# Interleaving the first two output chunks of an FFN's last slice, and closer spacing of a normalisation chain

## The chip, the cores and the metric

The kernel runs on one core of one Trainium2 chip. The metric is the device time of one execution in microseconds (us), lower is better. Engines are named as in the profile: PE is the matrix engine (PEld its weight loads), DVE the vector engine, ACT the scalar engine, POOL the general-purpose engine, SP the queue that issues most DMAs.

## What is computed

One inference step of a two-layer backbone over 640 tokens (512 latent tokens and 128 context tokens) of width 1024, in float32. Each layer is: half-step SwiGLU FFN, token mixer, half-step SwiGLU FFN. The mixer of layer 0 is a Fourier mix between two projections, that of layer 1 is 16-head attention. Every sub-layer stands between two RMS norms:

```
def _half_ffn(x, m, k, g_pre, g_post, w1, w2):
    h = _modulated_prenorm(x, g_pre, m, k)             # rmsnorm(x) * (1 + scale) + shift
    gate, up = split(h @ w1)
    return x + 0.5 * gate_k * _rmsnorm((silu(gate) * up) @ w2, g_post)
```

So there are six sub-layers, numbered n = 0 to 5: FFN, Fourier mix, FFN, FFN, attention, FFN. The FFN's hidden width is 2816, that is 22 tiles of 128.

## The kernel before

**Data.** Activations are kept transposed, 128 features by tokens, eight chunks of 128 features. The 640 tokens are worked as two halves of 320. A float32 product is made of three matmuls: weights and activations are each split into a high part (ACT copies it to the fast float32 format, `hi`) and the rest (DVE subtracts it, `lo`), and `mm3` (L228 to L230) issues hi by hi, hi by lo and lo by hi. Weights come in units of 128x1024: a DMA into one of four `raw` buffers (L156), ACT's `hi` (L194), DVE's `lo` (L195). `unit(i)` returns unit i and sends up to three units ahead of it.

**FFN.** The first product is made for hidden tiles f = 0 to 21, tiles 0 to 3 plainly, tiles 4 to 21 with a Strassen-like scheme that takes both halves at once (`w1_fast`). Of the last two tiles, 20 and 21, only half 0 is made at that point; their half 1 comes later (`tail`), from weight mixes that `mix` splits (L215, L216 on a 128x1024 `raw`). For half 0 of a tile, DVE subtracts the last product (L627), multiplies by the SiLU (L628), and `hidden` splits the result into g: ACT L215 for the high part, DVE L216 for the rest. The second product runs over slices of hidden tiles, (0,4), (4,8), (8,12), (12,16) and the last, (16,22). For each slice, half and output chunk m, `w2` takes a PSUM bank that ACT has seeded with the earlier slices' sum (L663), runs the tiles of the slice through `mm3`, and ACT copies the bank back to `y` (L675). In the last slice a chunk takes six tiles, 18 matmuls, the last three of which need g of tile 21. The slice has six weight units of eight 128x128 blocks; chunk m uses blocks 6m to 6m+5. The order of an FFN's end is: fast tiles 20 and 21, both mixes, reload of x, half 0 of the last slice (chunks 0 to 7), the boundary of half 0, `tail` for both tiles, half 1 of the last slice, the boundary of half 1.

**Boundary.** After each half a generator (`chain`: `post`, then the next sub-layer's `pre`) does the norms beside PE's next work. It is advanced by a clock that counts matmuls: `tick` adds 441.6 ns for a group of three 320-column matmuls, and each `yield n` says that the next piece is to be issued n ns of that clock later. Such a number only places the piece in program order: engines take their queues in order, and a list scheduler orders the queues at build time by that order and by its own estimate of when operands are ready. `post` issues: a fold of the sum of squares (L454) 2000 ns after the boundary, 1800 later a matmul that sums over partitions (L462), DVE's L465 and POOL's power (L466), 2800 later (2200 for half 0 and after a mixer) a matmul that spreads the result (L471) and ACT's copy of it (L475), 1300 later four pieces for two chunks each: DVE multiplies y by the norm (L520) and adds it to x (L522), ACT squares x (L420, L423) and DVE adds the squares (L424). Then `pre` does the same again for the next norm: fold L454, sum L462, spread L471, copy L475, and four pieces that scale x (L496, L502, L504) and split it into the next sub-layer's h (L215, L216). `finish(half)` or a loop of `step` issues what is left at once where the next sub-layer needs it. In attention two groups of value products (`v_tiles` for quads 1 and 0, "score" banks) stand behind half 0's query and key products; between them the chain is stepped until its second norm is through.

The few lines that fix this:

```
            yield 2500                       # in post, between the four pieces, L527/L528
...
            for f in range(f0, f1):          # in w2
                u, a = self.w2_tile(s, m, f - f0)
                w = self.unit(base + u)
```

`issue_after(x)` and `behind_of(x, y)` make the instructions that are built inside them stand behind x (and y) on x's (and y's) engine; no semaphore goes with it.

Of the kernel before, what the change touches and what calls it, by code (L numbers as in the profile page):

```python
# [24 lines left out]
HALF = TOK // 2  # L25
DEPTH = 2
DFF = 2816
NF = DFF // P
# [13 lines left out]
SLICES = ((0, 4), (4, 8), (8, 12), (12, 16), (16, 22))  # L42
# [10 lines left out]
SPAN = ((0, HALF), (HALF, TOK))  # L53
# [56 lines left out]
class Kernel:  # L110
# [271 lines left out]
    def gain_of(self, layer, sub, post):  # L382
        a = layer * 120 + 72 + (24 if post else 0) + sub * NCH
        return self.vec[:, a : a + NCH]
# [123 lines left out]
    def post(self, layer, sub, half, acc, last):  # L508

        nc = self.nc  # L510
        lo, hi = SPAN[half]
        r = yield from self.inverse_rms(acc, 2800 if half and sub != 1 else 2200)
        final = type(r) is tuple
        r, rp = r if final else (r, r)
        acc = None
        for c in range(0, NCH, 2):
            with self.tc.high_priority() if c == NCH - 2 else ExitStack():
                t = self.pair(self.y, c, half)
                engine, rb = (nc.gpsimd, r) if final and c == 2 else (nc.vector, rp)
                engine.tensor_tensor(t, t, rb[:, :HALF].unsqueeze(1).to_broadcast([P, 2, HALF]), op=ALU.mult)  # L520
                x = self.xpair(layer * 3 + sub + 1, c, half)
                engine.tensor_tensor(x, x, t, op=ALU.add)  # L522
                if last:
                    queue = nc.scalar if final and c == 2 else nc.sync
                    queue.dma_start(out=self.io["x_out"][:, c : c + 2, lo:hi], in_=x)
                else:
                    acc = self.sum_square(acc, x)  # L527
            yield 2500  # L528
        yield 1000
        self.normed[half][0] = True  # L530
        return acc

    def ffn(self, layer, which, base, boundary):
# [5 lines left out]
        g, sums, kept, mixes = {}, {}, {}, {}  # L539
        quad = lambda t: t.rearrange("p (c t) -> p c t", c=4)  # L540

        def hidden(f, v, half):
            lo, hi = SPAN[half]
            self.split(g[f][:, 0, lo:hi], g[f][:, 1, lo:hi], v[:, :HALF])

        def w1(fs, half):
            for f in fs:
                if f not in g:
                    g[f] = self.ring(F32R).rearrange("p (a t) -> p a t", a=2)
            pss = []  # L550
            if len(fs) == 1 or n == half == 0:
                for f in fs:
                    for j in range(2):
                        w = self.unit(base + self.w1_at[f] + j)
                        with self.tc.issue_after(self.latest.ins):
                            pss.append(self.proj(w, lambda k: k * P, half, kind="score" if f == 2 else "main"))
            else:
                pss = self.multi([self.unit(base + self.w1_at[f] + j) for f in fs for j in range(2)], half)
            for i, f in enumerate(fs):
                gate, up = pss[2 * i], pss[2 * i + 1]  # L560
                s, v = self.temp("left"), self.temp("right")
                with self.tc.high_priority():
                    nc.scalar.activation(s[:, :HALF], gate[:, :HALF], AF.Silu)
                    nc.vector.tensor_tensor(v[:, :HALF], up[:, :HALF], s[:, :HALF], op=ALU.mult)
                    hidden(f, v, half)
                while self.later:
                    self.later.pop()()
# [36 lines left out]
        def w1_fast(f):  # L604

            g[f] = self.ring(F32R).rearrange("p (a t) -> p a t", a=2)
            late = f in LATE
            a, q = (self.temp("left")[:, :HALF] for _ in range(2))
            s, v = (self.temp("right")[:, :HALF] for _ in range(2))
            x, y, z = (self.bank(kind)[:, :HALF] for kind in ("main", "score", "main"))  # L610
            product(f, x, 0, 0, lambda k: self.h.chunk(k, 0), True)
            with high():
                nc.scalar.activation(a, x, AF.Copy)
            product(f, y, 1, 512, lambda k: part(2, k), True)
            with high():
                tt(q, y, a, op=ALU.subtract)
            product(f, z, 1, 0, lambda k: part(3, k), True)
            with high():
                tt(a, q, z, op=ALU.subtract)
            if not late:  # L620
                w = one(f, a, 2)
            product(f, x, 0, 512, lambda k: self.h.chunk(4 + k, 0), False)
            with high():
                nc.scalar.activation(s, x, AF.Silu)
            product(f, z, 2, 0 if late else 512, lambda k: part(4, k), False)
            with high():
                tt(v, q, z, op=ALU.subtract)  # L627
                tt(v, v, s, op=ALU.mult)  # L628
                hidden(f, v, 0)
            if late:  # L630
                kept[f] = a, q
            else:
                two(f, a, q, w, 3, 0)
# [8 lines left out]
        def two(f, a, q, w, unit, at):  # L642
            product(f, w, unit, at, lambda k: self.h.chunk(4 + k, 1), False)
            with high():
                nc.vector.scalar_tensor_tensor(out=q, in0=w, scalar=-1.0, in1=q, op0=ALU.mult, op1=ALU.subtract)  # L645
                nc.scalar.activation(q, q, AF.Silu)
                tt(a, a, q, op=ALU.mult)
                hidden(f, a, 1)
# [7 lines left out]
        seeded = {}  # L656
# [5 lines left out]
            with self.tc.high_priority():  # L662
                nc.scalar.activation(ps[:, :HALF], self.y[:, m, lo:hi], AF.Copy)  # L663

        def w2(s, half, m):
            f0, f1 = SLICES[s]
            lo, hi = SPAN[half]
            ps = seeded.pop((s, half, m), None) or self.bank()
            for f in range(f0, f1):
                u, a = self.w2_tile(s, m, f - f0)  # L670
                w = self.unit(base + u)
                self.mm3(ps[:, :HALF], w[0][:, a : a + P], w[1][:, a : a + P],
                         g[f][:, 0, lo:hi], g[f][:, 1, lo:hi], f == f0 and s == 0, f == f1 - 1, s > 0)
            with self.tc.high_priority():
                nc.scalar.activation(self.y[:, m, lo:hi], ps[:, :HALF], AF.Copy)  # L675
            if f1 == NF:
                acc[half] = self.weigh(layer, 2 * which, half, m, acc[half])
# [3 lines left out]
        for op, a, half in self.ffn_plan:  # L681
# [3 lines left out]
            if op == "w1":  # L685
                if not begun[half]:
                    self.finish(half)
                    begun[half] = True
                w1(a, half)
            elif op == "combine":  # L690
                combine(a)
            elif op == "fast":
                w1_fast(a)
            elif op == "mix":
                mixes[a] = self.mix()
            elif op == "tail":
                tail(a)
            elif op == "w2":
                w2(a[0], half, a[1])
                if a[0] < len(SLICES) - 1:  # L700
                    passed += 1
                    due = BEHIND[n] * passed // (2 * NCH * (len(SLICES) - 1))
                    self.behind(due - done)
                    done = due
            elif op == "x":
                self.new_x(n + 1)
                for c in range(NCH // 2):
                    src = self.spilled[c].rearrange("p (c t) -> p c t", c=2) if n else self.io["x"][:, 2 * c : 2 * c + 2, :]
                    nc.sync.dma_start(out=self.xs[n + 1][c], in_=src)
            else:  # L710
                boundary(half, acc[half])
# [620 lines left out]
```

## Time and profile before

| what | value |
|---|---|
| time, median of 3 runs | 2305.4 us (2303.74 to 2306.14) |
| the profiled execution: its own time, its span | 2303.3 us, 2301.5 us |
| PE busy | 2253.5 us, 98% of the span |
| DVE, ACT, POOL busy | 75%, 56%, 2% |
| TensorE clock granted, mean | 0.995 |
| DMA over the span | 120 GB/s, 39275 instructions in all |

The span runs from the first to the last instruction. A row of the trace's timeline gives the start and the duration in us, the engine, the line, the operation, output and inputs, shapes, how many instructions are merged (x), and in brackets how long the engine had been idle and what released it.

### The profile page before, as it was taken

How to read it: one execution, taken by the hardware profiler on the slowest of the kernel's cores; microseconds unless marked ns; L12 is line 12 of the kernel's file. 1: busy time of each engine (PE TensorE's matmuls, PEld its weight loads, DVE VectorE, ACT ScalarE, POOL GpSimd, SP SyncE). 2: the span in 40 equal slices, each digit the busy share in tenths (PEclk: the TensorE clock that was granted, in tenths of full speed). 3: DMA queues.
4: the chain of work that ended last, by engine and by line, in shares of the span. 5: the costliest groups of instructions: out<-in, count | busy, mean ns of one | idle time of the engine just before them, and what ended most of it. 6: DMA issues, size and time to landing. Idle time of an engine off the chain costs nothing.

```text
span 2301.5 us, 39275 instructions
## 1 busy us (share of the span) xinstructions
PE 2253.5 (98%) x15660; PEld 2209.0 (96%) x15660; DVE 1732.4 (75%) x3010; ACT 1277.9 (56%) x2468; POOL 41.2 (2%) x64
## 2 busy tenths in 40 slices
PE   7999999999999999999999999999999999999997
PEld 5999999999999999999999999998888999999997
DVE  5889888588788887858978888578667485766574
ACT  5445544565654554556545554668668654545544
POOL 0000000000000000000000000000000000000000
PEclk9999999999999999999999999999999999999999
DMA  8244443334333433343334443424333223322331
GB/s 304 93 136 155 157 129 119 138 96 136 106 114 113 147 121 127 123 153 110 104 126 133 154 127 101 154 75 155 109 97 101 74 74 101 110 92 83 101 111 74
DMA packets 80281, 278.12 MB, mean 121 GB/s; under 512 B 8801, under 2 KB 15201, under 8 KB 79969
## 3 DMA queue, kind: packets, MB, share of 16 engines
q1 hardware_dynamic: 78736, 273.97, 36.3%
q8 instruction: 122, 2.00, 0.4%
q10 hardware_dynamic: 1360, 1.64, 0.2%
q14 instruction: 63, 0.51, 0.1%
HBM read 264.04 MB, written 11.53 MB: 120 GB/s over the span
## 4 chain that ended last, share of the span: by engine, by line
PE 88%; ACT 3%; DVE 3%; DMA 3%; issue 1%; POOL 0%; DVEq 0%; SPq 0%; ACTq 0%; POOLq 0%
PE main L228 25%; PE main L229 25%; PE main L230 25%; PE score L229 3%; PE score L230 3%; PE score L228 3%; DMA raw<-in_w 2%; DVE lo L195 1%; ACT hi L194 1%; PE turn L1147 1%; PE sum L1163 1%; PE sum L471 1%; PE score L1121 1%; PE sum L462 1%; ACT left L1107 0%
## 5 line engine op out<-in xcount | busy, mean ns | idle before, releaser
L228 PE MATMUL main<-ring,hi 128*128 128x320 f32 x3872 | 1205.2, 312 | 8.8 <-ACT ring L215 7.7
L229 PE MATMUL main<-ring,hi 128*128 128x320 f32 x3872 | 1198.1, 310 | 0.2 <-DVE ring L366 0.2
L230 PE MATMUL main<-ring,lo 128*128 128x320 f32 x3872 | 1197.6, 310 | 0.0
L228 PEld LDWEIGHTS main<-ring,hi 128*128 128x128 f32 x3872 | 727.6, 188 | 15.5 <-ACT ring L215 9.8
L229 PEld LDWEIGHTS main<-ring,hi 128*128 128x128 f32 x3872 | 728.5, 188 | 1.3 <-DVE ring L366 0.4
L230 PEld LDWEIGHTS main<-ring,lo 128*128 128x128 f32 x3872 | 728.0, 188 | 0.0
L194 ACT ACTIVATE hi<-raw 128x1024 fp32r<-128x1024 f32 (+1 forms) x366 | 355.8, 974 | 439.7 <-PE main L229 356.2
L195 DVE TENSOR_TENSOR lo<-raw,hi 128x1024 fp32r<-128x1024 f32 (+1 forms) x366 | 408.4, 1117 | 146.5 <-ACT hi L194 144.9
L388 DVE SCALAR_TENSOR_TENSOR junk<-raw,wide 128x1024 bf16<-128x1024 f32 x256 | 312.6, 1221 | 14.8 <-DMA raw<-in_w_mod_t 12.2
L675 ACT ACTIVATE y<-main 128x320 f32<-128x320 f32 x320 | 137.1, 432 | 154.0 <-PE main L230 153.3
L663 ACT ACTIVATE main<-y 128x320 f32<-128x320 f32 x256 | 111.4, 439 | 33.2 <-DVE left L645 26.8
L228 PE MATMUL score<-ring,hi 128*128 128x320 f32 x416 | 128.7, 309 | 0.0
L230 PE MATMUL score<-ring,lo 128*128 128x320 f32 x416 | 128.5, 309 | 0.0
L229 PE MATMUL score<-ring,hi 128*128 128x320 f32 x416 | 128.5, 309 | 0.0
L424 DVE TENSOR_TENSOR total<-total,square 128x640 f32<-128x640 f32 x71 | 58.4, 824 | 85.2 <-ACT square L423 83.8
L195 DVE TENSOR_TENSOR lo<-sums,hi 128x1024 fp32r<-128x1024 f32 x72 | 88.0, 1222 | 43.8 <-ACT hi L194 43.8
L194 ACT ACTIVATE hi<-sums 128x1024 fp32r<-128x1024 f32 x72 | 76.3, 1060 | 32.4 <-DVE sums L180 17.9
L228 PE MATMUL main<-ring,ring 128*128 128x320 f32 x288 | 90.9, 316 | 0.0
L230 PE MATMUL main<-ring,ring 128*128 128x320 f32 x288 | 89.1, 309 | 0.0
L229 PE MATMUL main<-ring,ring 128*128 128x320 f32 x288 | 89.0, 309 | 0.0
L215 ACT ACTIVATE ring<-right 128x320 fp32r<-128x320 f32 x104 | 47.9, 469 | 55.3 <-DVE right L628 34.4
L229 PEld LDWEIGHTS score<-ring,hi 128*128 128x128 f32 x416 | 78.1, 188 | 0.0
(185 smaller groups left out, 2631.3 us busy)
## 6 DMA issues: line engine op xcount, KB each, us to landing
raw<-in_w SPq DMA_DIRECT2D x264, 512.0 KB, 3.6
raw<-in_w_mod_t SPq DMA_DIRECT2D x128, 512.0 KB, 4.1
raw<-in_qkv SPq DMA_DIRECT2D x26, 512.0 KB, 3.6
first<-in_w_mod_k SPq DMA_DIRECT2D x16, 512.0 KB, 9.1
spill<-ring SPq DMA_DIRECT2D x12, 640.0 KB, 3.6
ring<-spill SPq DMA_DIRECT2D x12, 640.0 KB, 8.3
raw<-in_bias SPq DMA_DIRECT2D x16, 448.0 KB, 3.3
raw<-in_four_in SPq DMA_DIRECT2D x8, 512.0 KB, 3.7
```

The costliest lines, as they stand in the source:

```text
L194: nc.scalar.activation(hi, raw[:, at], AF.Copy)
L195: nc.vector.tensor_tensor(lo, raw[:, at], hi.bitcast(F32), op=ALU.subtract)
L215: a = self.nc.scalar.activation(hi, src, AF.Copy)
L228: mm(out, whi, xhi, start=start, stop=False)
L229: mm(out, whi, xlo, start=False, stop=False)
L230: self.latest = mm(out, wlo, xhi, start=False, stop=stop)
L388: last = self.nc.vector.scalar_tensor_tensor(out=self.junk, in0=raw, scalar=1.0, in1=self.wide[:, cond, :], op0=ALU.mult, op1=ALU.mult, ac ...
L424: nc.vector.tensor_tensor(acc, acc, sq, op=ALU.add)
L462: nc.tensor.matmul(ps[:, j : j + 1], acc[0][:, t : t + P], self.mean, start=True, stop=True)
L471: self.spread = nc.tensor.matmul(ps[:, t : t + P], col[:, j : j + 1].to_broadcast([P, P]), self.ident, start=True, stop=True)
L663: nc.scalar.activation(ps[:, :HALF], self.y[:, m, lo:hi], AF.Copy)
L675: nc.scalar.activation(self.y[:, m, lo:hi], ps[:, :HALF], AF.Copy)
```

## The change

Three edits. `hidden` keeps its two split instructions in `self.hid`. In the last slice, chunks 0 and 1 of half 0 are interleaved: first tiles 16 to 20 of chunk 0, then tiles 16 to 20 of chunk 1, then tile 21 of chunk 0, then tile 21 of chunk 1; chunks 2 to 7 and half 1 keep their order. The first part is built inside `behind_of(*self.hid)`, so weight units sent in it (the slice's fourth, and the fifth) stand behind tile 21's two split instructions on ACT and DVE. In `post`, half 1 of an FFN (sub 0 and 2) has 1800 instead of 2500 between its four pieces.

```
-            yield 2500
+            yield 1800 if half and sub != 1 else 2500
...
-            self.split(g[f][:, 0, lo:hi], g[f][:, 1, lo:hi], v[:, :HALF])
+            self.hid = self.split(g[f][:, 0, lo:hi], g[f][:, 1, lo:hi], v[:, :HALF])
...
+        def w2_part(ps, s, half, m, fs):
             f0, f1 = SLICES[s]
             lo, hi = SPAN[half]
-            ps = seeded.pop((s, half, m), None) or self.bank()
-            for f in range(f0, f1):
+            for f in fs:
                 u, a = self.w2_tile(s, m, f - f0)
                 w = self.unit(base + u)
                 self.mm3(ps[:, :HALF], w[0][:, a : a + P], w[1][:, a : a + P],
                          g[f][:, 0, lo:hi], g[f][:, 1, lo:hi], f == f0 and s == 0, f == f1 - 1, s > 0)
+
+        def w2(s, half, m):
+
+            f0, f1 = SLICES[s]
+            lo, hi = SPAN[half]
+            fs = range(f0, f1)
+            if f1 == NF and half == m == 0:
+                with self.behind_of(*self.hid):
+                    for i in range(2):
+                        w2_part(seeded[s, half, i], s, half, i, fs[:-1])
+            ps = seeded.pop((s, half, m), None) or self.bank()
+            w2_part(ps, s, half, m, fs[-1:] if f1 == NF and half == 0 and m < 2 else fs)
```

## Rows read from the trace of the kernel before

**Rows 1.** The page's busy time of PE, share of the span and instructions.

```profile
PE 2253.5 (98%) x15660; PEld 2209.0 (96%) x15660; DVE 1732.4 (75%) x3010; ACT 1277.9 (56%) x2468; POOL 41.2 (2%) x64
```

**Rows 2.** PE's waits over the span: us in total, times, longest.

```profile
PE main L228 <- ACT ring L215: 8.0, 6, 2.0
```

**Rows 3.** Timeline of PE around the start of each FFN's last slice.

```profile
424.47 0.31 PE L230 MATMUL main<-ring,lo 128*128 128x320 f32 x1
426.15 0.41 PE L228 MATMUL main<-ring,hi 128*128 128x320 f32 x1 [1.38 <-ACT ring L215]
...
1012.88 0.41 PE L228 MATMUL main<-ring,hi 128*128 128x320 f32 x1 [1.23 <-ACT ring L215]
...
1455.51 0.48 PE L228 MATMUL main<-ring,hi 128*128 128x320 f32 x1 [1.90 <-ACT ring L215]
...
2239.18 0.41 PE L228 MATMUL main<-ring,hi 128*128 128x320 f32 x1 [1.26 <-ACT ring L215]
```

**Rows 4.** Timeline of DVE at the first of these starts.

```profile
422.42 0.48 DVE L627 TENSOR_TENSOR right<-left,main 128x320 f32<-128x320 f32 x1
423.97 1.22 DVE L195 TENSOR_TENSOR lo<-raw,hi 128x1024 fp32r<-128x1024 f32 x1 [1.07 <-ACT hi L194]
425.11 0.48 DVE L628 TENSOR_TENSOR right<-right,right 128x320 f32<-128x320 f32 x1
426.13 0.49 DVE L216 TENSOR_TENSOR ring<-right,ring 128x320 fp32r<-128x320 f32 x1 [0.54 <-ACT ring L215]
```

**Rows 5.** Timeline of ACT at the first of these starts.

```profile
422.88 1.06 ACT L194 ACTIVATE hi<-raw 128x1024 fp32r<-128x1024 f32 x1 [1.30 <-DMA raw<-in_w]
...
425.63 0.47 ACT L215 ACTIVATE ring<-right 128x320 fp32r<-128x320 f32 x1 [1.37 <-DVE right L628]
426.01 1.04 ACT L215 ACTIVATE ring<-raw 128x1024 fp32r<-128x1024 f32 x1
```

**Rows 6.** Windows of equal length: busy time and count by engine, PEclk, DMA share, GB/s.

```profile
426.50:429.50 3.00, 3.00 (x22) 2.92 (x21) 2.49 (x3) 3.00 (x7) 0.00 (x0) 1.00 0.50 165
1455.70:1458.70 3.00, 3.00 (x12) 3.00 (x12) 2.54 (x3) 1.97 (x3) 0.00 (x0) 0.50 0.51 167
1534.40:1537.40 3.00, 2.83 (x13) 2.84 (x14) 2.15 (x6) 0.89 (x2) 0.00 (x0) 0.50 0.48 153
```

**Rows 7.** Timeline of PE where attention takes up half 1.

```profile
1527.54 0.28 PE L462 MATMUL sum<-mean,total 128*128 128x1 f32 x2
...
1529.67 0.38 PE L471 MATMUL sum<-ident,col 128*128 128x128 f32 x1 [0.49 <-POOL col L466]
...
1533.74 0.42 PE L228 MATMUL main<-ring,hi 128*128 128x320 f32 x1 [1.95 <-ACT ring L215]
```

**Rows 8.** Timeline of DVE at the same place.

```profile
1524.13 0.49 DVE L454 TENSOR_TENSOR total<-total 128x320 f32<-128x320 f32 x1
...
1531.11 0.83 DVE L496 TENSOR_TENSOR y<-ring,rms 128x640 f32<-128x640 f32 x1 [0.80 <-ACT rms L475]
...
1533.28 1.23 DVE L195 TENSOR_TENSOR lo<-raw,hi 128x1024 fp32r<-128x1024 f32 x1
```

**Rows 9.** Timeline of ACT at the same place.

```profile
1527.74 1.06 ACT L194 ACTIVATE hi<-raw 128x1024 fp32r<-128x1024 f32 x1 [0.38 <-PE score L230]
1530.64 0.44 ACT L475 ACTIVATE rms<-sum 128x320 f32<-128x320 f32 x1 [1.84 <-PE sum L471]
```

**Rows 10.** Timeline at the boundary into the third FFN: DVE and PE.

```profile
1085.25 0.48 DVE L454 TENSOR_TENSOR total<-total 128x320 f32<-128x320 f32 x1
...
1085.94 0.30 PE L462 MATMUL sum<-mean,total 128*128 128x1 f32 x2
...
1088.31 0.38 PE L471 MATMUL sum<-ident,col 128*128 128x128 f32 x1 [0.93 <-POOL col L466]
```

**Rows 11.** Timeline at the boundary into the Fourier mix: DVE and PE.

```profile
497.77 0.49 DVE L454 TENSOR_TENSOR total<-total 128x320 f32<-128x320 f32 x1
...
498.41 0.24 PE L462 MATMUL sum<-mean,total 128*128 128x1 f32 x1
```

More of the change, by code (lines that the diff above doesn't have):

```diff
@@ L663, in seed @@
                 nc.scalar.activation(ps[:, :HALF], self.y[:, m, lo:hi], AF.Copy)
-        def w2(s, half, m):
+        def w2_part(ps, s, half, m, fs):
             f0, f1 = SLICES[s]
             lo, hi = SPAN[half]
-            ps = seeded.pop((s, half, m), None) or self.bank()
-            for f in range(f0, f1):
+            for f in fs:
                 u, a = self.w2_tile(s, m, f - f0)
```

## Prediction, made before the change was built or run

> **What bounds the kernel now.** I read the page first: PE is busy 98% of the span [rows 1], so a gain must come from PE's pauses or from a better clock, and work on DVE, ACT or the DMAs counts only where PE waits for it. The waits of PE come next: the largest group after start-up is L228 waiting for ACT's split (L215), 8.0 us in six waits [rows 2]. The timeline of PE places four of the six: the start of the last slice in each of the four FFNs, 1.38, 1.23, 1.90 and 1.26 us idle [rows 3]. The matmul that ends the idle time is the first that needs g of tile 21. A fifth, 1.95 us, is where attention takes up half 1 [rows 7].
>
> The idle time is counted from the modelled end of the matmul before, 0.31 us after its start [rows 3], while matmuls in a stream start 0.147 us apart (441.6 ns for three on the kernel's own clock). So a pause costs PE its idle time plus 0.16 us: 1.54, 1.39, 2.06 and 1.42, together 6.4 us, and 2.1 us in attention.
>
> The reason for the first four stands in the queues of DVE and ACT. At the first FFN, DVE has finished L627 by 422.9 and could do L628 at once, but L195 of a weight unit stands between them; it runs from 423.97 to 425.19, and only then come L628, the high part and the rest [rows 4]. That L195 waited for ACT's L194, and this for its DMA, at 422.88 [rows 5]. It is the slice's fourth unit, the one that the slice's first call of `unit` sends three ahead: blocks 24 to 31, wanted first by chunk 4. So a unit that is wanted four chunks later holds up tile 21.
>
> **Part 1, the interleaving.** It adds no matmul and removes none. PE has 15 matmuls (2.2 us) between the last product of tile 21 and the first use of its g; after the change it has 30, 4.4 us. In the first FFN the use falls due at 424.47 + 0.15 = 424.62 before, at 426.8 after. With the old queues the rest of g is there at 426.62 [rows 4]; the four pauses (1.39 to 2.06) are all shorter than the added 2.2 us. The interleaving alone thus covers all four. Chunk 0's bank is copied out 2.2 us later and chunk 1's at the same place in the order; the bank that chunk 0 gives back is wanted by chunk 4, two chunks (5.3 us) later.
>
> **Part 2, the fourth unit behind tile 21.** L628 then follows L627: it starts near 423.0, and by the spacings in the rows (0.52 to the high part, 0.50 to the rest, 0.49 long) g is complete at 424.5, 2.3 us ahead of the new use and even about in time for the old. What is late next: the unit's L194 and L195 move behind the split, so its low part ends near 425.7 in place of 425.19. It is wanted by chunk 4, at 422.4 + 4 x 2.65 = 433.0; 7 us are left. On SP's queue a load waits for this unit's raw buffer, that of the sixth unit (wanted by chunk 6, near 440), and behind it stand the next sub-layer's loads and the reload of x, all for users later still: 0.5 us more costs none of them. The fifth unit already ran behind the split. The mix of 1.04 us on ACT that follows the split [rows 5] may slip ahead of it, with as much on DVE as a unit's L195, 1.22 [rows 4]: inside the 2.3 us. I put the loss at 0. Parts 1 and 2 give 6.4 us.
>
> **The clock.** After the third pause, the longest, the granted clock is 0.5 (1.2 GHz, the lower of the two levels): 12 matmuls in 3 us; after attention's pause the same. After the first, shorter pause it stays at 1.00, with 22 matmuls [rows 6]. Such a stretch thus costs 10 matmuls of 0.147 us, 1.5 us. The pause gone, I expect the stretch gone with it: 1.5 us from the third FFN. The Trainium skill speaks against this, on its page "TensorE: Matmul & The Clock Gate", Part 1, "What's actually happening": there it is idleness of the whole window looked at that brings the lower clock back. By that rule a pause with work close on both sides is not the cause, and the sum would lack this term; the rows, in which the two falls stand right behind the two longest pauses, do not agree with it.
>
> **Part 3, 1800 for 2500.** The first, sum, spread and copy keep their places; the pieces of `post` stand at 7.9, 9.7, 11.5 and 13.3 us after the boundary (before: 7.9, 10.4, 12.9, 15.4), and the closing sum of `pre` at 17.9 in place of 20.7. No work is added. The chain stands 2.8 us earlier in program order; whether it runs earlier depends on DVE's fold (L454).
>
> In attention it can. The fold is done at 1524.6 [rows 8], but the sum runs at 1527.54 [rows 7]: it is due 20.7 after the boundary and the first group of value products ends at 14.1 + 5.65 = 19.8, so it comes behind them (32 groups of three at 0.4416 us for the products, 16 at 0.353 for the values), and spread, copy (1530.64 [rows 9]), L496 and the rest follow late. With 17.9 the sum falls inside that group, near 1527.54 - 1.9 = 1525.6, after the fold. POOL's power then runs beside matmuls, and the spread follows the group at once, some 1.4 us earlier than the 1529.67 of now. This can remove the 2.1 us pause, the 0.49 + 0.16 before the spread, and the half clock behind it (1.5): 4.2 us at most. Against the whole of it: the second value group needs the low part of a weight unit, whose L194 waits for PE to free a buffer (1527.74 [rows 9]) and whose L195 stands at 1533.28 in DVE's queue behind L496 [rows 8]. If L195 keeps its place behind L496 it ends 1.4 us earlier, like all behind the spread, while PE comes to it 1.1 us earlier, and most of the pause stays. But L195 could run from 1528.8, when its high part is there, and DVE sits idle for 0.80 us before L496 even now [rows 8]. Bounds 0 and 4.2; I take 3.0, nearer to the upper end, since a pause only a little shorter may already keep the clock.
>
> At the third FFN the fold ends at 1085.73, PE's sum follows at 1085.94, and the spread then waits 0.93 us for POOL [rows 10]; at the Fourier mix the fold ends at 498.26 and the sum follows at 498.41 without a wait [rows 11]. In both the sum already follows the fold closely, so the fold, not the interval, sets it. Earlier pieces let DVE finish the fold earlier by something up to 2.8 us, or not at all. No PE wait for h follows either. Gain at most 1.1 (the wait for POOL and its edge), loss see below; I take +0.3. In the last FFN nothing runs behind the chain, so the spacing places nothing.
>
> **The sum.** 6.4 + 1.5 + 3.0 + 0.3 = 11.2 us. The profiled execution took 2303.3 us, 1.8 more than its span, and lies 2.1 us under the median of the runs, just below the fastest of them (2303.74). Its own time becomes 2292.1, the median of runs 2305.4 - 11.2 = 2294.2.
>
> **The rivals.**
> *A. Attention's wait is only renamed.* The low part of the value unit takes the place of h, and the clock falls as before: 6.4 + 1.5 + 0.65 (the wait before the spread) = 8.55, 2296.9. For it: L195's place behind L496 [rows 8]. Against: DVE's half 0 work moves ahead too.
> *B. The earlier sums stall PE: slower than before.* PE takes its queue in order. If the sums at the Fourier mix and the third FFN are placed 2.8 us earlier and the folds end where they do now, PE waits 498.26 - 495.6 = 2.7 and 1085.73 - 1083.1 = 2.6 us, each long enough for a half-clock stretch as after the 1.90 and 1.95 us pauses: 2 x (2.65 + 1.5) = 8.3 against 7.9 gained, 2305.8, and more if DVE's fold is pushed back by the crowding. It decides from the point where both pauses reach 2.5 us. Against it: the queues' order puts both sums right behind the folds now, so the scheduler's estimate of the folds is good there, and DVE's pieces, issued earlier, should end earlier.
> *C. The first four pauses stay,* because something else than the fourth unit is late. Part 3 alone gives 3.3: 2302.1. Against: two independent covers.
> *D. The clock falls without the pauses,* at times of its own: neither the third FFN nor attention gets its 1.5 us back, 6.4 + 1.5 (part 3 without the clock) + 0.3 = 8.2, 2297.2. Against it: two falls, both behind a pause [rows 6, 7]. The rule of the Trainium skill cited above would be a reason for it.
>
> **How the numbers follow.** Forecast (all four pauses gone, attention partly or wholly) 0.66; A 0.14; B 0.09; C 0.05; D 0.06. The forecast's own range is 2290.5 to 2298: all gains at their upper bounds, 6.4 + 1.5 + 4.2 + 1.1 = 13.2, give 2292.2, less 1.6 for a half-clock stretch that other runs may have had more; the upper end is part 3 at nothing (2297.5). A and D lie inside it; B begins above it. Range 2289.5 to 2300.5, the upper end being parts 1 and 2 with a loss of 3 at the folds. Faster by over 0.2% (4.6 us, about what a measurement of this kernel can tell from no change) means under 2300.8: forecast, A, D and a third of B less some doubt, 0.85. Within 0.2%: C and most of B, 0.11. Slower: 0.04, for a crowding of DVE that no row prices.
>
> **What would show it.** PE's first last-slice use of g without idle time in all four FFNs; chunk 0's five tiles followed by chunk 1's; L627, L628 and L216 within 2.1 us with the fourth unit's L195 behind; no half clock after the third; in attention the sum L462 inside the first value group, some 2 us earlier relative to it, and the pause before half 1's products shorter. A wait of L462 for L454 at the Fourier mix or the third FFN would show B. The prediction is wrong if a new PE wait over 1 us appears elsewhere, above all in attention, where DVE's order follows from the chain's place.

## Result and the profile after

The changed kernel takes 2291.7 us (median of four runs, 2291.64 to 2293.24) beside 2305.3 us for the kernel before in the same rounds (2303.74 to 2306.14): a ratio of 0.9945, 95% interval 0.9933 to 0.9957. The profiled execution took 2291.65 us by itself (before: 2303.3), its span is 2289.9 us, the mean granted clock 0.996. The forecast was 2294.2 in a range of 2289.5 to 2300.5.

The page's busy time by engine, as in [rows 1]:

```profile
PE 2249.0 (98%) x15660; PEld 2206.2 (96%) x15660; DVE 1731.3 (76%) x3010; ACT 1276.1 (56%) x2468; POOL 41.3 (2%) x64
```

PE has the same 15660 matmuls; its pauses have changed. Its waits over the span, largest first (total us, times, longest):

```profile
PE turn L316 <- DMA first<-in_w_mod_k: 13.0, 5, 6.8
PE turn L1158 <- ACT right L1160: 5.8, 13, 0.8
PE sum L471 <- POOL col L466: 2.1, 2, 1.2
...
PE score L229 <- DVE lo L195: 1.4, 2, 1.3
```

The 8.0 us for ACT's split of [rows 2] are gone from the list. The last line has grown. It is a score product that waits for the low part of a weight unit, and the kernel before has it with 0.4 us:

```profile
PE score L229 <- DVE lo L195: 0.4, 2, 0.3
```

Of the 1.4 us now, 1.26 are one wait in attention, near the place of [rows 7]. DVE at the first FFN's last slice, answering to [rows 4]:

```profile
421.55 1.23 DVE L195 TENSOR_TENSOR lo<-raw,hi 128x1024 fp32r<-128x1024 f32 x1 [2.77 <-ACT hi L194]
422.69 0.48 DVE L627 TENSOR_TENSOR right<-left,main 128x320 f32<-128x320 f32 x1
423.20 0.49 DVE L628 TENSOR_TENSOR right<-right,right 128x320 f32<-128x320 f32 x1
424.23 0.49 DVE L216 TENSOR_TENSOR ring<-right,ring 128x320 fp32r<-128x320 f32 x1 [0.54 <-ACT ring L215]
425.18 1.23 DVE L216 TENSOR_TENSOR ring<-raw,ring 128x1024 fp32r<-128x1024 f32 x1 [0.46 <-ACT ring L215]
426.33 1.22 DVE L195 TENSOR_TENSOR lo<-raw,hi 128x1024 fp32r<-128x1024 f32 x1
```

L628 follows L627 at once, g of tile 21 is complete at 424.72 (before: 426.62), and the fourth unit's L195 comes behind it, after a mix. The first line is the L195 of the weight unit sent before that one. It still stands ahead of L627, in the kernel before as in the change and in all four FFNs, and L627 starts only as it ends, 1.4 to 2.1 us behind tile 21's last product. PE reaches the first use of that g without idle time:

```profile
425.48 0.31 PE L230 MATMUL main<-ring,lo 128*128 128x320 f32 x1
425.63 0.31 PE L228 MATMUL main<-ring,hi 128*128 128x320 f32 x1
```

Windows of 3 us at the third FFN's last slice (two) and in attention, to be read beside the 12 and 13 matmuls at a clock of 0.50 in [rows 6]:

```profile
1448.60:1451.60 3.00, 3.00 (x23) 3.00 (x22) 2.00 (x3) 2.92 (x5) 0.00 (x0) 1.00 0.54 175
1452.00:1455.00 3.00, 3.00 (x22) 3.00 (x22) 2.29 (x3) 3.00 (x7) 0.00 (x0) 1.00 0.73 237
1524.00:1527.00 3.00, 2.83 (x24) 2.63 (x23) 2.97 (x8) 1.71 (x4) 0.00 (x0) 1.00 0.74 208
```

PE in attention, and at the boundary into the third FFN:

```profile
1084.94 0.94 PE L471 MATMUL sum<-ident,col 128*128 128x128 f32 x6 [0.92 <-POOL col L466]
...
1518.65 0.73 PE L462 MATMUL sum<-mean,total 128*128 128x1 f32 x6
...
1521.12 0.83 PE L471 MATMUL sum<-ident,col 128*128 128x128 f32 x6
...
1523.33 0.39 PE L229 MATMUL score<-lo,ring 128*128 128x256 f32 x1 [1.26 <-DVE lo L195]
...
1525.19 0.39 PE L229 MATMUL score<-lo,ring 128*128 128x256 f32 x1 [0.17 <-DVE lo L195]
```

The wait of 0.93 us at the third FFN [rows 10] is still 0.92. In attention the sum L462 now runs inside the first value group and the spread L471 follows that group without a wait; then PE waits for L195.

**Where the time went.** Subtracting the start of PE's n-th matmul in one trace from that in the other gives a running difference, which steps up where a pause shrank:

| place | gained, us | forecast, us |
|---|---|---|
| first, second, fourth FFN's last slice | 1.72 + 1.58 + 1.61 = 4.91 | 1.54 + 1.39 + 1.42 = 4.35 |
| third FFN's last slice: pause, then behind it | 2.07 + 1.63 = 3.70 | 2.06 + 1.5 = 3.56 |
| attention | 3.4 | 3.0 |
| third FFN's boundary, Fourier mix, the rest | -0.3 | 0.3 |
| sum | 11.7 | 11.2 |

In the last row 0.43 are gained in the Fourier mix, where the sixth wait of [rows 2], 0.29 us, is gone in the change and in every experiment; the forecast gave it no price. Small steps elsewhere, 0.13 of them in the start-up, more than take this back. The third FFN's boundary gives nothing.

The profiled executions differ by 11.65 us. The medians differ by 13.6, since the profiled execution of before lies at the fast end of its runs.

### The profile page after: what moved, and what is told of

Same layout as the page of the kernel before. It is cut to its first block, busy times and chain, and to the rows that moved or that the text cites. A ratio compares the mean times of both kernels' runs of the same rounds, so it can differ in the third digit from the quotient of the medians.

```text
span 2289.9 us, 39281 instructions
## 1 busy us (share of the span) xinstructions
PE 2249.0 (98%) x15660; PEld 2206.2 (96%) x15660; DVE 1731.3 (76%) x3010; ACT 1276.1 (56%) x2468; POOL 41.3 (2%) x64
## 4 chain that ended last, share of the span: by engine, by line
PE 93%; ACT 3%; DVE 2%; DMA 1%; issue 1%; POOL 0%; DVEq 0%; SPq 0%; ACTq 0%
PE main L228 27%; PE main L229 26%; PE main L230 26%; PE score L229 3%; PE score L228 3%; PE score L230 3%; PE turn L1158 1%; PE sum L1174 1%; PE sum L462 1%; PE score L1132 1%; PE sum L471 1%; ACT left L1118 1%; ACT right L1160 1%; DMA first<-in_w_mod_k 0%; ACT left L1152 0%
## 5 line engine op out<-in xcount | busy, mean ns | idle before, releaser
L194 ACT ACTIVATE hi<-raw 128x1024 fp32r<-128x1024 f32 (+1 forms) x366 | 355.9, 974 | 435.1 <-PE main L229 359.8
L195 DVE TENSOR_TENSOR lo<-raw,hi 128x1024 fp32r<-128x1024 f32 (+1 forms) x366 | 408.1, 1116 | 143.1 <-ACT hi L194 141.8
L195 DVE TENSOR_TENSOR lo<-sums,hi 128x1024 fp32r<-128x1024 f32 x72 | 87.9, 1221 | 43.2 <-ACT hi L194 43.2
L194 ACT ACTIVATE hi<-sums 128x1024 fp32r<-128x1024 f32 x72 | 76.3, 1060 | 31.3 <-DVE sums L180 16.8
L228 PEld LDWEIGHTS score<-ring,hi 128*128 128x128 f32 x416 | 78.1, 188 | 0.0
L229 PEld LDWEIGHTS score<-ring,hi 128*128 128x128 f32 x416 | 78.1, 188 | 0.0
```

Source lines behind the costliest of these rows:

```text
L194: nc.scalar.activation(hi, raw[:, at], AF.Copy)
L195: nc.vector.tensor_tensor(lo, raw[:, at], hi.bitcast(F32), op=ALU.subtract)
L228: mm(out, whi, xhi, start=start, stop=False)
L229: mm(out, whi, xlo, start=False, stop=False)
```

## Experiments

The kernel before, run beside them, had medians of 2305.4 to 2306.9. Its single executions spread over 2302.1 to 2309.1 us, so gains of 1 to 2 us are read from the traces here, and the medians say only whether a whole part counts.

**The interleaving alone.** Without the order behind the split, with 2500 everywhere:

```
-                with self.behind_of(*self.hid):
-                    for i in range(2):
-                        w2_part(seeded[s, half, i], s, half, i, fs[:-1])
+                for i in range(2):
+                    w2_part(seeded[s, half, i], s, half, i, fs[:-1])
```

> Only the interleaving: chunks 0 and 1 built as in the change, without the order behind tile 21's split, intervals 2500. Theory Q (the queue of before had already put 24 matmuls, chunk 0's and part of chunk 1's, ahead of the first use of tile 21; the interleaving makes it 30, 0.88 us more): the four pauses stay, shorter by 0.88 us each, about 0.66, 0.51, 1.18 and 0.54 us, 2.9 in all; L195 of the fourth unit still stands between L627 and L628; with the third pause down to 1.2 us the half-clock stretch behind it should go: 6.4 - 2.9 + 1.5 = 5.0 us gained, about 2300.3. Theory C (the prediction's: cover rises from 15 to 30 matmuls, enough for all four by itself): no pauses, 7.9 us gained, about 2297.4.

Measured: 2300.55 us (2298.69 to 2304.12), ratio 0.9977 (0.9967 to 0.9988), span 2297.4. PE at the first, third and fourth FFN, then DVE at the first:

```profile
426.81 0.42 PE L228 MATMUL main<-ring,hi 128*128 128x320 f32 x1 [1.07 <-ACT ring L215]
...
1453.84 0.41 PE L228 MATMUL main<-ring,hi 128*128 128x320 f32 x1 [0.90 <-ACT ring L215]
...
2235.68 0.42 PE L228 MATMUL main<-ring,hi 128*128 128x320 f32 x1 [0.68 <-ACT ring L215]
```

```profile
422.58 0.48 DVE L627 TENSOR_TENSOR right<-left,main 128x320 f32<-128x320 f32 x1
424.63 1.23 DVE L195 TENSOR_TENSOR lo<-raw,hi 128x1024 fp32r<-128x1024 f32 x1 [1.56 <-ACT hi L194]
425.77 0.48 DVE L628 TENSOR_TENSOR right<-right,right 128x320 f32<-128x320 f32 x1
```

The unit's L195 still stands between L627 and L628, g is no earlier than before, and PE still waits for it, only shorter. The forecast that the interleaving alone covers all four pauses is wrong. The order in which PE's instructions stand in the two programs shows why. Each line is a group of three matmuls (bank, tile of g), right after tile 21's own product:

```
before                          after
chunk 0, tiles 16 to 20 (5)     chunk 0, tiles 16 to 20 (5)
chunk 1, tiles 16, 17, 18 (3)   chunk 1, tiles 16 to 20 (5)
chunk 0, tile 21                chunk 0, tile 21
chunk 1, tiles 19, 20, 21       chunk 1, tile 21
```

(In the left column the groups of chunk 0's tile 21 and chunk 1's tile 19 are mixed matmul by matmul.) The program's list scheduler had interleaved the two chunks already, against the order of the source: eight groups, 24 matmuls, stood ahead of the first use in each of the four FFNs. The written interleaving adds two groups, 6 x 0.147 = 0.88 us, not 2.2.

**The order behind the split alone.** Only chunk 0's five tiles are built inside `behind_of`, and chunk 1 starts after tile 21:

```
                 with self.behind_of(*self.hid):
-                    for i in range(2):
-                        w2_part(seeded[s, half, i], s, half, i, fs[:-1])
+                    w2_part(seeded[s, half, 0], s, half, 0, fs[:-1])
...
```

> Only the order behind tile 21's split: chunk 0's five tiles are built behind it, chunk 1 is built whole after chunk 0, intervals 2500. In this build PE's queue has 18 matmuls ahead of the first use of tile 21. Theory Q: L627, L628, L215 and L216 follow each other as in the trace of the change, but the use falls due 12 matmuls (1.76 us) earlier than there: pauses of about 0.75, 0.55, 0.75 and 1.2 us are left, 3.2 in all, no half clock: 6.4 + 1.5 - 3.2 = 4.7 us gained, about 2300.6. Theory U (the fourth unit is the whole cause, cover does not matter): no pauses, 7.9 us gained, about 2297.4.

Measured: 2297.58 us (2297.15 to 2298.98), ratio 0.9963 (0.9951 to 0.9976), span 2297.2. PE at the first and the fourth FFN, and DVE at the first:

```profile
424.51 0.42 PE L228 MATMUL main<-ring,hi 128*128 128x320 f32 x1 [0.48 <-ACT ring L215]
...
2233.03 0.41 PE L228 MATMUL main<-ring,hi 128*128 128x320 f32 x1 [1.22 <-ACT ring L215]
```

```profile
422.95 0.48 DVE L627 TENSOR_TENSOR right<-left,main 128x320 f32<-128x320 f32 x1
423.47 0.49 DVE L628 TENSOR_TENSOR right<-right,right 128x320 f32<-128x320 f32 x1
424.49 0.49 DVE L216 TENSOR_TENSOR ring<-right,ring 128x320 fp32r<-128x320 f32 x1 [0.54 <-ACT ring L215]
```

DVE's chain is as short as in the change, but in this order only 17 matmuls stand ahead of the first use (the 18 of the expectation is one too many), since two matmuls of chunk 1 get in between instead of nine. Idle times of 0.48, 0.12 and 1.22 us remain at the first, third and fourth FFN and none at the second. At the fourth the unit sent earlier is the late one, which this order doesn't move; DVE there, right ahead of L627:

```profile
2230.33 1.23 DVE L195 TENSOR_TENSOR lo<-raw,hi 128x1024 fp32r<-128x1024 f32 x1 [3.31 <-ACT hi L194]
```

The span is 4.3 us shorter; the medians fall by 8.4, which the section on the prediction comes back to. In these two builds neither half suffices: the order takes 1.9 us off g, the interleaving gives PE the work to bridge what is left. But this build also took away the cover of the old queue. With the old 24 matmuls and the g times of the changed kernel's trace, the use would have fallen due at 424.75 in the first FFN (its low part one matmul later, at 424.90), with g complete at 424.72. Reckoned alike, g is in time in the second and third and 0.3 us late in the fourth. So the order alone, with the old queue kept, might have covered nearly all; this is an estimate, and no run has that build.

**The slice without the norm chain's spacing:** both parts, 2500 everywhere.

```
-            yield 1800 if half and sub != 1 else 2500
+            yield 2500
```

> Interleaving and order behind tile 21's split, intervals 2500. Theory Q and the prediction's sum agree: no pause at the four last slices, no half clock after the third, attention's pause of 2 us and its half clock as before: 7.9 us gained, about 2297.4. Rival: the half-clock stretches come at times of their own, so the one after the third pause comes back elsewhere: 6.4 us, 2298.9.

Measured: 2296.27 us (2296.08 to 2296.44), ratio 0.9955 (0.9943 to 0.9968), span 2294.4. No last-slice pause is left. Windows behind the place of the old third pause, and in attention:

```profile
1450.50:1453.50 3.00, 3.00 (x22) 3.00 (x21) 2.90 (x3) 3.00 (x7) 0.00 (x0) 1.00 0.39 119
1528.30:1531.30 3.00, 3.00 (x16) 3.00 (x16) 2.37 (x9) 0.93 (x2) 0.00 (x0) 0.50 0.50 153
```

The half clock is gone where the pause is gone and stays in attention, where the pause of 1.9 us stays. Rival D, a clock that falls at times of its own, has lost its ground.

**The spacing alone:** the kernel before with `yield 1800 if half and sub != 1 else 2500`.

> Only 1800 for 2500 in the second half's chain; the last slice as before. If the parts add up: attention's pause before half 1 and its half-clock stretch go, a pause of about 1.5 us for the value unit's low part comes, as in the trace of the change: 3.3 us gained, about 2302.0; the four pauses at the last slices and the half clock after the third stay. Rival: what attention gains hangs on the earlier parts (the place of the clock's fall, DVE's queue): no gain, 2305.3.

Measured: 2303.8 us (2300.89 to 2304.55), ratio 0.9986 (0.9977 to 0.9995), span 2302.1. PE at the four last slices and in attention, then windows behind each of the four:

```profile
427.65 0.56 PE L228 MATMUL main<-ring,hi 128*128 128x320 f32 x2 [1.85 <-ACT ring L215]
...
1015.57 0.56 PE L228 MATMUL main<-ring,hi 128*128 128x320 f32 x2 [1.17 <-ACT ring L215]
...
1458.36 0.56 PE L228 MATMUL main<-ring,hi 128*128 128x320 f32 x2 [2.08 <-ACT ring L215]
...
1533.38 0.39 PE L229 MATMUL score<-lo,ring 128*128 128x256 f32 x1 [1.26 <-DVE lo L195]
...
2239.05 0.56 PE L228 MATMUL main<-ring,hi 128*128 128x320 f32 x2 [1.68 <-ACT ring L215]
```

```profile
429.20:432.20 3.00, 3.00 (x13) 3.00 (x12) 1.74 (x2) 2.50 (x6) 0.00 (x0) 0.50 0.45 142
1016.00:1019.00 3.00, 3.00 (x22) 2.92 (x22) 2.40 (x3) 3.00 (x7) 0.00 (x0) 1.00 0.54 169
1460.00:1463.00 3.00, 3.00 (x13) 3.00 (x12) 1.66 (x2) 2.61 (x7) 0.00 (x0) 0.50 0.46 149
2239.50:2242.50 3.00, 3.00 (x22) 2.92 (x21) 2.39 (x3) 3.00 (x7) 0.00 (x0) 1.00 0.84 306
```

Attention gains 3.4 us as in the change, with the wait for L195 of 1.26 us. The last slices, whose queues are those of before, took longer in this execution than in [rows 3], the second apart, and two of them drew a half clock. That the medians gain less (2.2 us) than attention's 3.4 fits this.

**The spacing only in front of attention:** the change with one condition narrowed.

```
-            yield 1800 if half and sub != 1 else 2500
+            yield 1800 if half and (layer, sub) == (1, 0) else 2500
```

> The change, with 1800 only for the chain into attention; the chains into the Fourier mix and the third FFN and the last one keep 2500. Theory S (only attention gains: in the trace of the change the closing fold there lies 17.2 and 17.9 us behind the chain's first power step, as before, so DVE sets it and not the interval): the same time as the change, 2291.7 within 0.5 us. Rival: the two other chains gained too: at least 0.5 us slower than the change.

Measured: 2291.89 us (2291.26 to 2293.67), ratio 0.9945 (0.9931 to 0.9958), as the whole change. At the other boundaries the shorter interval does nothing that these runs show.

**The two waits that remain.** One experiment sets the low part of the first key chunk behind the low part of the value unit on DVE, so that PE's new wait in attention loses its cause:

```
-                    put(slice(2))
+                    put(slice(1))
+                with self.behind_of(self.summed, self.squared, self.low[early["v1", 0]]):
+                    put(slice(1, 2))
```

> The change, and in attention the low part of the first key chunk on DVE stands behind the low part of the second value group's weight units. Theory L (the pause of about 1.5 us left in attention is the value unit's low part waiting behind DVE's key pieces): the pauses of 1.3 us and 0.3 us at the value products go, and half 1's products come without a pause: 1.5 to 1.8 us less than the change, about 2290.0. Rival H: the wait goes over to h, since L496 and what follows it run later: a pause of 1 to 2 us before half 1's products, no gain, 2291.7 or more with a half-clock stretch.

Measured: 2290.23 us (2289.73 to 2291.07), ratio 0.9936 (0.9924 to 0.9949). DVE in attention after the change, and with this edit:

```profile
1519.68 0.99 DVE L965 SCALAR_TENSOR_TENSOR ring<-main,ring 64x320 fp32r<-64x320 f32 x2
1520.69 1.33 DVE L984 TENSOR_TENSOR ring<-main,ring 64x128 fp32r<-64x128 f32 x4
1522.04 1.23 DVE L195 TENSOR_TENSOR lo<-raw,hi 128x1024 fp32r<-128x1024 f32 x1
```

```profile
1520.24 0.99 DVE L965 SCALAR_TENSOR_TENSOR ring<-main,ring 64x320 fp32r<-64x320 f32 x2
1521.54 1.23 DVE L195 TENSOR_TENSOR lo<-raw,hi 128x1024 fp32r<-128x1024 f32 x1 [0.30 <-ACT hi L194]
...
1524.33 0.82 DVE L496 TENSOR_TENSOR y<-ring,rms 128x640 f32<-128x640 f32 x1
```

With L984 out of the way L195 starts 0.5 us earlier by the traces' clocks. PE stands 0.56 us further back in this trace when it enters attention's value products, so against PE it is 1.06 us, and PE's wait falls from 1.26 to 0.19:

```profile
1522.82 0.39 PE L229 MATMUL score<-lo,ring 128*128 128x256 f32 x1 [0.19 <-DVE lo L195]
```

By the traces this is 1.5 us less than the change, and all of it is gained there. So the wait that the change left in attention was one of DVE's order, as theory L has it.

The other wait is the spread's 0.92 us for POOL at the third FFN. An argument of the root's step was raised to leave more room between sum and spread there: from 2200 to 3600, on the change and on the edit above,

```
-        r = yield from self.inverse_rms(acc, fold=fold)
+        r = yield from self.inverse_rms(acc, 3600 if half and n == 3 else 2200, fold)
```

> The change, with 3600 for 2200 between sum and spread in the norm ahead of the third FFN's second half. Theory P (PE waits 0.93 us there only because the spread is placed four groups' worth of matmuls too early for POOL): the wait goes, PE goes on with matmuls in its place: 1.1 us less than the change, about 2290.6. Rival: the later spread makes h late for half 1: a pause of PE before half 1 instead, no gain, 2291.7.

> The two last edits together on top of the change. If theories L and P both hold: 2.6 to 2.9 us less than the change, about 2289.0; if L falls and P holds 2290.6; if L holds and P falls 2290.0; if both fall 2291.7.

Measured: 2292.26 us (0.9944, 0.9931 to 0.9956), and with both edits 2289.96 (0.9935, 0.9923 to 0.9948). These two tell nothing of theory P: the spread still stands four matmuls behind the sum in PE's order, as in the change, and the wait is there as ever. PE's waits around this boundary in the first of the two:

```profile
PE sum L471 <- POOL col L466: 0.9, 1, 0.9
```

With 6000 and the key part behind:

> The kernel with the key part behind the value unit, and 6000 instead of the 3600 tried before between sum and spread in the norm ahead of the third FFN's second half. With 3600 PE's queue had not changed there, since the sum itself stands later than that; with 6000 the spread stands 13 matmuls behind the sum instead of 4. Theory P (the pause is only the spread's place in PE's queue): PE's wait for POOL, 1.1 us lost, goes, and h is as early as now: 1.1 us less than the kernel with the key part behind (2290.2), about 2289.1. Rival: half 1 comes to wait for h, which is no earlier: a pause of the same size before half 1's products, no gain.

Measured: 2290.43 us, ratio 0.9931 (0.9917 to 0.9944). Now the spread stands 13 matmuls behind the sum and POOL's wait is gone, but h comes later:

```profile
1090.41 0.42 PE L229 MATMUL main<-ring,hi 128*128 128x320 f32 x1 [0.28 <-DVE ring L216]
```

Against the kernel with the key part behind, the trace shows 1.1 us gained and 0.4 given back, which the time (2290.43 beside 2290.23) doesn't show.

**More cover instead of the order.** The first experiment with three chunks interleaved (three banks seeded), so that 45 matmuls stand ahead of the first use while the unit keeps its place:

```
-                    for i in range(2):
+                for i in range(3):
...
-                while adds and len(seeded) < 2 and adds[0][0] == a[0]:
+                while adds and len(seeded) < (3 if a == (len(SLICES) - 1, 0) and half == 0 else 2) and adds[0][0] == a[0]:
```

> Only more cover: chunks 0, 1 and 2 interleaved in the last slice (three banks seeded), 45 matmuls ahead of the first use of tile 21 in place of 30; the fourth weight unit keeps its place between L627 and L628; intervals 2500. Theory Q: the pauses left with 30 matmuls (0.5 to 1.6 us) are shorter than the 2.2 us of added cover, so all four go, without the order behind the split: like the slice edits alone, 9.7 us under the median of the kernel before by the same call's runs, 2296.3. Rival R: the queue entry of the fourth unit also delays something else that PE waits for (a bank, a weight unit), so pauses stay: 2298 to 2300.

Measured: 2294.72 us (2292.4 to 2296.39), ratio 0.9952 (0.9939 to 0.9964), span 2294.6. DVE at the first FFN:

```profile
422.54 0.48 DVE L627 TENSOR_TENSOR right<-left,main 128x320 f32<-128x320 f32 x1
424.44 1.23 DVE L195 TENSOR_TENSOR lo<-raw,hi 128x1024 fp32r<-128x1024 f32 x1 [1.42 <-ACT hi L194]
425.58 0.49 DVE L628 TENSOR_TENSOR right<-right,right 128x320 f32<-128x320 f32 x1
```

The unit stands where it stood, L628 starts no earlier than in the kernel before (425.11 [rows 4]), and yet PE waits for tile 21 in none of the four FFNs. So the unit's place is not needed where the cover is long enough: what matters is the number of matmuls ahead of the first use against the time that g takes. The third bank costs a new wait, in the fourth FFN:

```profile
2238.39 0.42 PE L228 MATMUL main<-ring,hi 128*128 128x320 f32 x1 [0.52 <-ACT main L663]
```

## Why the prediction held, and the step that failed

**What bounds the kernel** was read rightly: PE, and of its pauses those for ACT's split. The price of a pause, its idle time plus 0.16 us, holds: at the pauses themselves the difference steps by 1.54, 1.39, 2.07 and 1.42 us, for 1.54, 1.39, 2.06 and 1.42. Where the clock stays, another 0.18 us come back in the six matmuls right behind the pause, which the sum lacked. In the kernel before these six, of two banks mixed, start 0.26, 0.14, 0.14, 0.24 and 0.14 us apart at the first FFN; in the change the groups follow each other and the starts are 0.147 us apart.

**Part 1 failed.** It says that PE has 15 matmuls between tile 21's product and the first use of its g, 30 after, and that the interleaving thus covers all four pauses by itself. The 15 came from the order of the source. PE's queue held 24, the interleaving adds 0.88 us in place of 2.2, and alone it leaves pauses of 1.07, 0.90 and 0.68 us in the first, third and fourth FFN. The trace of before held the answer: the use fell due at 424.62 and tile 21's last product starts at 420.95,

```profile
420.95 0.31 PE L230 MATMUL main<-ring,lo 128*128 128x320 f32 x1
```

and the 3.67 us between them hold 24 matmuls and the step to the next, not 15. That the total did not suffer was luck for part 1, as part 2 held up. The second cover that the text counts against rival C was a thin one: without part 2 the span fell by 4.1 us, of which 1.5 are the third FFN's clock, so some 2.6 of the 6.4 us went and 3.8 stayed. Rival C, in which all four stay, is thereby half true for part 1 by itself, and wrong for the two together.

**Part 2** was right in mechanism and nearly in numbers: g was forecast complete at 424.5 and was at 424.72. The slack ahead of the use, forecast as 2.3 us, is 425.63 - 424.72 = 0.9 for the same miscount, and 1.1, 0.9 and 0.4 in the other three FFNs. It leaves out the other unit, whose L195 stands ahead of L627 and sets when the split can begin. A mix did slip in ahead of the unit's L195 (425.18), as the text allowed, and nobody waits for the unit: the loss is 0.

**The clock** came back as forecast: behind the third pause 1.63 us, less the 0.18 that came back behind the others too, is 1.45 for 1.5. It fell in no stretch of the changed kernel but at its start and its end, it stayed whole at the third FFN where the pause was shortened to 0.90 us (the interleaving alone), and it fell at two last slices in the execution in which two of their pauses were longest (the spacing alone). By the Trainium skill's rule cited in the prediction ("TensorE: Matmul & The Clock Gate", Part 1, "What's actually happening"), a pause with work close on both sides should not cost the clock; the traces here do not agree, and by it the gain would have been 1.5 us less at the third FFN and as much in attention.

**Part 3** gained in attention what was taken from between its bounds, 3.4 us for 3.0. The mechanism is a mixture of the forecast and rival A. The sum moved into the first value group, and the waits before the spread and for h went. The value unit's low part did take the place of h, as A said, with a pause of 1.26 us. The prediction names a new PE wait over 1 us, above all in attention, as a sign that it is wrong, and this is one. Its reason for such a wait was not the one found: L195 did not keep its place behind L496, it runs ahead of it (1522.04 before 1523.19), but behind the key pieces L984. That the clock would fall as before is what A had wrong. The pause of 1.95 became 1.26 and the clock stayed at 1.00, the reason for which 3.0 was chosen. Which wait ends last behind a removed one was visible [rows 8]; its size was not.

**The other boundaries** gave nothing for the 0.3. Rival B did not come: the fold sets the sums there, not the interval. In both traces the closing fold ends 17.2 us (Fourier mix) and 17.9 us (third FFN) behind the start of the chain's first L465, so issuing the pieces closer moves nothing. That the narrowed spacing has the time of the whole change bears this out.

**The medians** fell by 13.6 us and not by 11.2, partly since the traces show 11.7, and mostly because the kernel before varies, over 7 us in all its runs, while the changed one stays within 1.6. The forecast's sum comes from one execution, which lies 2.0 us under the median of its runs; its range set 1.6 us aside for half-clock stretches that other runs may have had. The versions that leave the fourth unit ahead of tile 21's split vary over 2.4 to 7 us, those that put it behind over 0.4 to 2.8.

The traces say what makes the old pauses longer or shorter. With the spacing alone, where the queues of the last slices are as before, one execution showed 1.85, 1.17, 2.08 and 1.68 us and two half clocks. ACT at its first FFN, answering to [rows 5]:

```profile
424.37 1.06 ACT L194 ACTIVATE hi<-raw 128x1024 fp32r<-128x1024 f32 x1 [1.72 <-DMA raw<-in_w]
```

PE's first use follows this start by 3.28 us, and by 3.27 in the kernel before (426.15 - 422.88). It is 3.27 or 3.28 in all eight last slices of the two traces, and in all eight L194 had waited for its DMA. So the landing of the unit's DMA sets the length of these pauses. The clock goes with the time as well: of the 36 executions of the kernel before beside the experiments, the two with a mean granted clock of 0.996 took 2302.1 and 2302.7 us, the eleven with 0.992 took 2306.3 to 2309.1. That later transfers and half clocks behind longer pauses make the whole spread fits this, but single executions without a trace don't show it, and three interleaved chunks, without a pause at tile 21 in the trace, still vary over 4.0 us.

## What to carry to other kernels

Count the cover of a late operand in the queue of the engine, not in the source: a list scheduler may have spent it already, and the number of matmuls between two starts in the trace gives it away. A split of a weight that waits for its transfer holds up everything behind it on ACT and DVE, so place it behind the work that PE wants next, and look at what that leaves as the last wait. When a chain is issued closer, it gains only where the interval and not an operand sets its place; here that was one boundary of three.

## What was not expected of the hardware

The lower clock (0.50, 1.2 GHz) went here with how long PE had paused, by a small margin. Away from the kernel's start and end it followed every pause of 1.85 us or more in these traces (1.85, 1.90, 2.08, and 1.94 or 1.95 in five), with matmuls on both sides; none followed 1.17, 1.23, 1.26, 1.38 or 1.68 us. No run changed the length of a pause and nothing else. Such a stretch behind a last slice holds 12 or 13 matmuls in 3 us instead of 22 and costs some 1.5 us, not much less than the pause itself. In attention, where a pause of 1.26 us took the place of one of 1.95, the stretch went too.
